# Dilated queries and keys of a two-layer hybrid attention kernel: transposed as 32-bit rows of two heads, split afterwards

## The chip, the cores and the metric

The kernel runs on one core of one Trainium2 chip. The metric is device time in microseconds (us), the median of the runs of one kernel. The engines are called by their names here; in the profile they are PE (TensorE), PEld (TensorE's weight loads), DVE (VectorE), ACT (ScalarE), POOL (GpSimd) and SP (SyncE, which issues all the DMAs that this text speaks of).

## The reference, cut to what matters

Two layers, each on 2048 tokens of width 1024. A layer normalizes its input, multiplies it with one weight matrix and cuts the result into queries, keys, values and gates of two attentions: stick-breaking (4 heads of 64) and dilated windows (12 heads of 64, three patterns). The part that matters is the road from the projection to the dilated attention:

```python
qd = _partial_rope(_rmsnorm(heads(qd, N_HEADS_DIL), q_norm_g[layer]), pos)
kd = _partial_rope(_rmsnorm(heads(kd, N_HEADS_DIL), k_norm_g[layer]), pos)
od = _dilated_mixture(qd, kd, heads(vd, N_HEADS_DIL))
```

`_rmsnorm` divides each head's 64 values by their root mean square and multiplies them with a gain, `_partial_rope` rotates the first 16 of them by the token's position. `_dilated_mixture` then needs scores of queries against keys, so both must lie with the head's 64 values on the partitions.

## The kernel before, in words

The sequence is cut into 16 token tiles of 128. Products of float32 precision are made from float32r matmuls: each operand is split into a rounded high part and the rest, and three products are summed (`mm3`, lines 310 to 312, 128x512 each here).

In a layer `Project.run` works through blocks of 512 columns of the weights: one of stick-breaking queries and keys ("sq"), three of dilated ones ("qk": 256 columns of queries and 256 of keys, so 4 heads of each), then values and gates. A block is 8 groups of two token tiles; a group is 8 x 3 = 24 matmuls for each tile, 48 in all, into two PSUM banks (ring `pm`, four banks). So there are 3 x 8 = 24 "qk" groups in a layer and 48 in the kernel. At the end of a block the next block's weights are loaded (line 228) and split (lines 234 on ScalarE, 235 on VectorE), two k steps at a time, in two raw buffers.

Each "qk" group ends in `qk_out`. The square of the projection (ScalarE, line 361) and its sum over a head (VectorE, 362) give the norm, GpSimd makes the reciprocal root (135, 138), VectorE multiplies (366), GpSimd multiplies with the gain (371) and rotates (378 to 381) in the SBUF tile `qn`, which holds 2 token tiles x 8 heads x 64 values. Then, for each token tile, ScalarE rounds `qn` into the high half of a tile `q2` (line 385) and VectorE writes the rest into its low half (386), so that a head's 64 high and 64 low values lie side by side. For each head and token tile TensorE transposes these 128 columns (line 395), which puts high over low on the partitions, four transposes into one PSUM bank (ring `pt`, four banks). Four evictions follow (397, two on VectorE and two on ScalarE) and four DMAs (399) into the DRAM scratch `qk_scr[pair, 2 queries + 2 keys, 128, 2048]`. The dilated attention reads that scratch later (lines 657 to 666).

The order on each engine is not written out here: a scheduler fixes it before the run from a simulated timeline of the whole kernel, with the exception of the attentions' TensorE work, which is pinned to program order. Waits between engines are semaphores.

Of the kernel before, what the change touches and what calls it, by code (L numbers as in the profile page):

```python
# [10 lines left out]
F32 = mybir.dt.float32  # L11
F32R = mybir.dt.float32r
BF16 = mybir.dt.bfloat16
AF = mybir.ActivationFunctionType
ALU = mybir.AluOpType
# [14 lines left out]
def _constants():  # L30
# [16 lines left out]
    for run, r in ((32, 4), (8, 16)):  # L47
        q = (r * np.arange(run)[None, :] + np.arange(r)[:, None]).reshape(-1)
        cols += [mask(q, q - 128), mask(q, q)]
# [140 lines left out]
class Project:  # L190
# [96 lines left out]
    def run(self, sq_scr, sb_scr, v_scr, qk_scr, g_scr, inject):  # L287
        nc, mem = self.tc.nc, self.mem
# [4 lines left out]
        pm, pt = self.pm, self.pt  # L293
# [7 lines left out]
        r2 = xa[:, 768:1024].rearrange("p (a b c) -> p a b c", a=2, c=16)  # L301
        stg = mem.ring("S0", "S1")
        qnr = mem.ring("H2", "H3")
        q2r = mem.ring("H4", "H5")
        qsr = mem.ring("H0", "H1")
        ssr = mem.ring("U2", "U3")

        def mm3(ps, c, k, wh, wl):
# [48 lines left out]
        def qk_out(i, pss, c):  # L357
            qn = qnr.get([128, 2, 8, 64])
            ss = ssr.get([128, 16])
            for j, ps in enumerate(pss):  # L360
                nc.scalar.activation(qn[:, j].rearrange("p b d -> p (b d)"), ps, AF.Square)
            nc.vector.tensor_reduce(out=ss, in_=qn.rearrange("p a b d -> p (a b) d"),  # L362
                                    op=ALU.add, axis=mybir.AxisListType.X)
            self.rstd_of(ss, ss, 64)
            for j, ps in enumerate(pss):
                nc.vector.tensor_tensor(
                    out=qn[:, j], in0=ps.rearrange("p (b d) -> p b d", d=64),
                    in1=ss[:, 8 * j:8 * j + 8].unsqueeze(2).to_broadcast([128, 8, 64]), op=ALU.mult)
            for s in range(2):
                v = qn[:, :, 4 * s:4 * s + 4]  # L370
                nc.gpsimd.tensor_tensor(
                    out=v, in0=v,
                    in1=gain[:, s].unsqueeze(1).unsqueeze(1).to_broadcast([128, 2, 4, 64]), op=ALU.mult)

            def tb(s, lo, n):
                return tab[:, s, c:c + 2, lo:lo + n].unsqueeze(2).to_broadcast([128, 2, 8, n])

            nc.gpsimd.tensor_tensor(out=r1, in0=qn[:, :, :, 0:16], in1=tb(0, 0, 16), op=ALU.mult)
            nc.gpsimd.tensor_tensor(out=r2[:, :, :, 0:8], in0=qn[:, :, :, 8:16], in1=tb(1, 0, 8), op=ALU.mult)
            nc.gpsimd.tensor_tensor(out=r2[:, :, :, 8:16], in0=qn[:, :, :, 0:8], in1=tb(1, 8, 8), op=ALU.mult)  # L380
            nc.gpsimd.tensor_tensor(out=qn[:, :, :, 0:16], in0=r1, in1=r2, op=ALU.add)
            q2 = []
            for j in range(2):
                t = q2r.get([128, 8, 2, 64], F32R)
                nc.scalar.copy(t[:, :, 0], qn[:, j])
                nc.vector.tensor_tensor(out=t[:, :, 1], in0=qn[:, j], in1=t[:, :, 0].bitcast(F32),
                                        op=ALU.subtract)
                q2.append(t)
            for s in range(2):
                st = qsr.get([128, 2, 2, 256])  # L390
                for m in range(2):
                    ps = pt.get([128, 2, 2, 128], F32R)
                    for h in range(2):
                        for j in range(2):
                            nc.tensor.transpose(ps[:, h, j],  # L395
                                                q2[j][:, 4 * s + 2 * m + h].rearrange("p s d -> p (s d)"), self.ident_r)
                    (nc.scalar.copy if m else nc.vector.tensor_copy)(
                        st[:, m].rearrange("p h t -> p (h t)"), ps.bitcast(F32).rearrange("p h j t -> p (h j t)"))
                    nc.sync.dma_start(
                        out=qk_scr[2 * i + m, 2 * s:2 * s + 2, :, 128 * c:128 * c + 256].rearrange("g p t -> p g t"),  # L400
                        in_=st[:, m])

        self.wt.update({p: mem.get(p, [128, 2048], F32R) for p in ("F2", "F3")})
        wide = [("sq", 0, [(0, QA, 512)])]
# [28 lines left out]
        for bi, (kind, idx, parts) in enumerate(wide):  # L433
            nxt = wide[bi + 1][2] if bi + 1 < len(wide) else None
            for g in range(NT // 2):
# [20 lines left out]
                if kind == "qk":  # L456
                    qk_out(idx, pss, 2 * g)
                    continue
# [3 lines left out]
                for j, ps in enumerate(pss):  # L462
                    st = stg.get([128, 512])
# [3 lines left out]
        for bi, (kind, idx, parts) in enumerate(tail):  # L467
# [9 lines left out]
            for gi, (ct, tq) in enumerate(order):  # L477
# [3 lines left out]
                t = slice(512 * tq, 512 * tq + 512)  # L481
                ps = pm.get([128, 512])
                for k in range(NK):
                    mmw(ps, ct, tq, k, wh[:, k], wl[:, k])
                g = stg.get([128, 512])
# [140 lines left out]
def _dilated(tc, mem, v_scr, qk_scr, g_scr, mix, masks, sel, ident, neg1):  # L626
# [87 lines left out]
    def front(g):  # L714
# [7 lines left out]
        if p:  # L722
            run, stp = (32, 4) if p == 1 else (8, 1)
            w0 = 0 if first else run * (n - 1)
# [262 lines left out]
```

## Time and profile before

| | |
|---|---|
| median of 3 runs | 3177.85 us (3176.13 to 3178.02) |
| profiled execution, own time | 3175.44 us |
| its span, first to last instruction | 3173.7 us |
| mean granted TensorE clock | 0.992 |
| TensorE busy | 3100.5 us, 98% |
| VectorE, ScalarE, GpSimd busy | 51%, 45%, 38% |
| "qk" transposes in the trace, line 395 | 189.7 to 475 us and 1769 to 2054.4 us |

Times of the trace count from the first instruction's start. A row of a timeline has the start in us, the duration in us, the engine, the line of the kernel, the operation, the tiles written and read, and the number of instructions merged into the row; in brackets the idle time before it and what ended it. Matmuls overlap in their pipeline and their ends are modelled, so TensorE's pace is read from one start to the next.

### The profile page before, as it was taken

The page shows a single profiled execution, that of the slowest core. Times are in us where ns is not written, and L with a number is a line of the kernel's source. Part 1 is how long each engine was busy: PE and PEld are TensorE (multiplying, and loading weights), DVE is VectorE, ACT ScalarE, POOL GpSimd, SP SyncE. Part 2 cuts the span into 40 slices and gives each one's busy share as a digit, 9 for nine tenths or more (in the row PEclk, how much of TensorE's full clock was granted, in tenths as well). Part 3 has the DMA queues.
Part 4 walks back from the last instruction along what each step waited for, and adds up shares of the span by engine and source line. Part 5 has one row for each costly group of instructions (what it writes and reads, how often), then busy time and mean ns, then how long its engine had stood idle before and what let it go on. Part 6 is the DMA issues. An engine that isn't in the chain of part 4 may idle for free.

```text
span 3173.7 us, 58878 instructions
## 1 busy us (share of the span) xinstructions
PE 3100.5 (98%) x21712; PEld 2643.9 (83%) x21712; DVE 1618.6 (51%) x4131; ACT 1425.4 (45%) x4013; POOL 1201.7 (38%) x1302
## 2 busy tenths in 40 slices
PE   8999999999999999989999999999999999999899
PEld 8888888987778998868898888888878789888787
DVE  6234440013777888875252344401147778788721
ACT  5223331113667888852042233311136678888410
POOL 1057761002663444451010677511026634454500
PEclk9999999999999999999999999999999999999899
DMA  6333346416223566354443233464162235663443
GB/s 201 91 96 114 112 131 189 129 63 195 75 88 107 151 175 187 114 160 148 125 140 109 90 107 115 145 186 126 50 202 73 89 104 151 194 173 105 145 146 104
DMA packets 313823, 413.15 MB, mean 130 GB/s; under 512 B 20160, under 2 KB 245440, under 8 KB 303296
## 3 DMA queue, kind: packets, MB, share of 16 engines
q1 hardware_dynamic: 313536, 409.38, 42.2%
q8 instruction: 173, 2.83, 0.4%
q14 instruction: 114, 0.93, 0.1%
HBM read 252.01 MB, written 157.29 MB: 129 GB/s over the span
## 4 chain that ended last, share of the span: by engine, by line
PE 87%; DVE 4%; POOL 2%; issue 2%; ACT 2%; DMA 2%; SPq 0%; DVEq 0%; POOLq 0%; ACTq 0%
PE b L311 9%; PE b L310 9%; PE b L312 9%; PE b L737 8%; PE b L772 6%; PE b L758 6%; PE b L316 6%; PE b L318 6%; PE b L317 6%; PE b L940 4%; PE b L941 4%; PE b L937 4%; PE b L597 4%; PE b L583 2%; PE b L395 2%
## 5 line engine op out<-in xcount | busy, mean ns | idle before, releaser
L743 ACT ACTIVATE H<-H,T 128x256 f32<-128x256 f32 (+1 forms) x1152 | 519.3, 455 | 80.6 <-DVE T L739 75.8
L739 DVE CUSTOM_DVE_ANT_0 H<-b,M 128x256 f32<-128x256 f32 (+1 forms) x1152 | 371.0, 360 | 109.6 <-PE b L758 41.4
L737 PE MATMUL b<-F,F 128*128 128x256 f32 (+1 forms) x2304 | 408.2, 301 | 2.8 <-DVE T L739 2.8
L312 PE MATMUL b<-F,F 128*128 128x512 f32 (+1 forms) x1152 | 409.2, 355 | 0.4 <-DVE F L283 0.3
L565 DVE TENSOR_TENSOR_SCAN G<-G,b 128x513 f32<-128x513 f32 (+3 forms) x320 | 324.6, 1079 | 84.8 <-ACT G L564 69.0
L571 POOL TENSOR_TENSOR G<-G 128x512 f32<-128x512 f32 (+3 forms) x320 | 287.9, 913 | 190.8 <-DVE G L565 154.7
L737 PEld LDWEIGHTS b<-F,F 128*128 128x128 f32 x2304 | 312.1, 191 | 31.7 <-issue 26.3
L758 PE MATMUL b<-ident,H 128*128 128x128 f32 x1800 | 298.3, 277 | 5.1 <-ACT H L760 2.6
L311 PE MATMUL b<-F,G 128*128 128x512 f32 (+1 forms) x768 | 274.6, 358 | 0.0
L310 PE MATMUL b<-F,G 128*128 128x512 f32 (+1 forms) x768 | 274.2, 357 | 0.0
L311 PE MATMUL b<-F,F 128*128 128x512 f32 (+1 forms) x768 | 273.4, 356 | 0.0
L310 PE MATMUL b<-F,F 128*128 128x512 f32 (+1 forms) x768 | 272.1, 354 | 0.0
L312 PEld LDWEIGHTS b<-F,F 128*128 128x128 f32 x1152 | 217.6, 189 | 30.8 <-DVE F L283 0.8
L760 DVE COPY H<-b 128x512 f32<-128x512 f32 (+1 forms) x432 | 241.5, 559 | 1.2 <-PE b L758 0.9
L135 POOL TENSOR_SCALAR U<-U 128x16 f32<-128x16 f32 (+1 forms) x80 | 33.1, 414 | 535.5 <-DVE U L362 315.2
L772 PE MATMUL b<-H,H 128*64 128x128 f32 x3600 | 235.8, 278 | 0.0
L317 PE MATMUL b<-F,F 128*128 128x512 f32 x576 | 224.5, 390 | 0.0
L564 ACT ACTIVATE G<-b 128x512 f32<-128x512 f32 (+3 forms) x320 | 164.0, 558 | 133.0 <-PE b L557 105.8
L758 PEld LDWEIGHTS b<-ident,H 128*128 128x128 f32 x1800 | 211.7, 141 | 14.4 <-ACT H L743 6.1
L772 PEld LDWEIGHTS b<-H,H 128*64 128x64 f32 x3600 | 193.2, 137 | 32.0 <-issue 22.4
L743 ACT ACTIVATION_READ_ACCUMULATOR H<-H,T 128x1 f32 x1152 | 219.3, 190 | 0.0
L487 DVE TENSOR_TENSOR S<-b,S 128x512 f32<-128x512 f32 x64 | 44.3, 692 | 318.8 <-ACT S L486 318.8
(159 smaller groups left out, 6636.4 us busy)
## 6 DMA issues: line engine op xcount, KB each, us to landing
qk_l<-H SPq DMA_DIRECT2D x192, 256.0 KB
F<-qk_l SPq DMA_DIRECT2D x48, 1024.0 KB
v_l<-S SPq DMA_DIRECT2D x288, 128.0 KB
H<-v_l SPq DMA_DIRECT2D x72, 512.0 KB
F<-qk_l SPq DMA_DIRECT2D x48, 512.0 KB
sq_l<-H SPq DMA_DIRECT2D x64, 256.0 KB
g_l<-S SPq DMA_DIRECT2D x64, 256.0 KB
F<-sq_l SPq DMA_DIRECT2D x32, 512.0 KB
```

The lines of the kernel that those rows point to most:

```text
L310: nc.tensor.matmul(ps, hT(q, 0, k)[:, cs], wh, start=k == 0, stop=False)
L311: nc.tensor.matmul(ps, hT(q, 0, k)[:, cs], wl, start=False, stop=False)
L312: nc.tensor.matmul(ps, hT(q, 1, k)[:, cs], wh, start=False, stop=k == NK - 1)
L317: nc.tensor.matmul(ps, wh[:, w], hT(tq, 1, k), start=False, stop=False)
L565: nc.vector.tensor_tensor_scan(out=r[:, 0:n + 1][:, ::-1], data0=g[:, 512 - n:513][:, ::-1], data1=z[:, 0:1].to_broadcast([128, n + 1]), i ...
L571: nc.gpsimd.tensor_tensor(out=b[:, :n], in0=r[:, 1:n + 1], in1=r[:, 0:n], op=ALU.subtract)
L737: pin(nc.tensor.matmul(sc[:, h, :un], qb, kv, start=s == 0, stop=s == 1))
L739: nc.vector.tensor_tensor_reduce(out=pe[:, h, :un], in0=sc[:, h, :un], in1=mk[:, m0:m0 + un], scale=-0.125, scalar=3.0e38, op0=ALU.add, op ...
L743: nc.scalar.activation(pe[:, h, :un], pe[:, h, :un], AF.Exp, scale=-1.0, bias=st[:, 0, p, h, b:b + 1], accum_out=st[:, 1, p, h, b:b + 1])
L758: pin(nc.tensor.transpose(tp[:, ch, h], pe[:, h, 128 * w:128 * w + 128], ident))
L760: (nc.scalar.copy if g % 4 == 1 else nc.vector.tensor_copy)(ts[:, :nch], tp[:, :nch])
L772: pin(nc.tensor.matmul(ob[64 * h:64 * h + 64, b % 4], vq[(pr * 3 + p) * 2 + (b - ch) // 8][:, (b - ch) % 8, 64 * h:64 * h + 64], ts[:, ch, h],
```

## The change: what it does

`qn` is no longer split. TensorE transposes it as plain float32, with the float32 identity: 128 columns are now two heads of 64, for one token tile. A group makes 8 such transposes, four into each of two PSUM banks. The split is made when a bank is evicted: ScalarE's copy rounds to the high part `hi`, VectorE subtracts it from the bank and gets `lo`. Each DMA takes 64 partitions (one head) of `hi` or `lo` for two pairs and writes it to the rows where the scratch wants it, high over low; there are eight of these in a group, each of 64 x 2 x 256 values. The scratch has the same content and layout as before. The buffers H4 and H5, which held `q2`, now make up the second halves of the rings of `hi` and `lo`.

```diff
-        q2r = mem.ring("H4", "H5")
-        qsr = mem.ring("H0", "H1")
+        qsr = mem.ring("H0", "H4")
+        qsl = mem.ring("H1", "H5")
...
-            q2 = []
-            for j in range(2):
-                t = q2r.get([128, 8, 2, 64], F32R)
-                nc.scalar.copy(t[:, :, 0], qn[:, j])
-                nc.vector.tensor_tensor(out=t[:, :, 1], in0=qn[:, j], in1=t[:, :, 0].bitcast(F32),
-                                        op=ALU.subtract)
-                q2.append(t)
             for s in range(2):
-                st = qsr.get([128, 2, 2, 256])
+                hi, lo = qsr.get([128, 2, 256], F32R), qsl.get([128, 2, 256], F32R)
+                ps = pt.get([128, 2, 2, 128])
                 for m in range(2):
-                    ps = pt.get([128, 2, 2, 128], F32R)
-                    for h in range(2):
-                        for j in range(2):
-                            nc.tensor.transpose(ps[:, h, j],
-                                                q2[j][:, 4 * s + 2 * m + h].rearrange("p s d -> p (s d)"), self.ident_r)
-                    (nc.scalar.copy if m else nc.vector.tensor_copy)(
-                        st[:, m].rearrange("p h t -> p (h t)"), ps.bitcast(F32).rearrange("p h j t -> p (h j t)"))
-                    nc.sync.dma_start(
-                        out=qk_scr[2 * i + m, 2 * s:2 * s + 2, :, 128 * c:128 * c + 256].rearrange("g p t -> p g t"),
-                        in_=st[:, m])
+                    for j in range(2):
+                        nc.tensor.transpose(ps[:, m, j], qn[:, j, 4 * s + 2 * m:4 * s + 2 * m + 2].rearrange(
+                            "p h d -> p (h d)"), self.ident)
+                pv = ps.rearrange("p m j t -> p m (j t)")
+                nc.scalar.copy(hi, pv)
+                nc.vector.tensor_tensor(out=lo, in0=pv, in1=hi.bitcast(F32), op=ALU.subtract)
+                for l, x in enumerate((hi, lo)):
+                    for h in range(2):
+                        nc.sync.dma_start(
+                            out=qk_scr[2 * i:2 * i + 2, 2 * s + h, 64 * l:64 * l + 64,
+                                       128 * c:128 * c + 256].rearrange("m p t -> p m t"),
+                            in_=x[64 * h:64 * h + 64].bitcast(F32))
```

## Rows read from the trace of the kernel before

**Rows 1.** The page: span; busy time, share and instructions of TensorE.

```profile
span 3173.7 us, 58878 instructions
...
PE 3100.5 (98%) x21712; PEld 2643.9 (83%) x21712; DVE 1618.6 (51%) x4131; ACT 1425.4 (45%) x4013; POOL 1201.7 (38%) x1302
```

**Rows 2.** Busy by stretch: length, engines' us (instructions), granted clock, DMA share, GB/s.

```profile
180.00:480.00 300.00, 300.00 (x1552) 251.24 (x1552) 136.75 (x191) 94.58 (x167) 206.67 (x191) 1.00 0.35 113
1760.00:2060.00 300.00, 300.00 (x1553) 251.25 (x1552) 136.95 (x191) 95.69 (x167) 205.97 (x191) 1.00 0.34 113
```

**Rows 3.** The chain of waits, 399 to 427 us: shares by line.

```profile
by line: PE b L312 29.2%; PE b L311 29.1%; PE b L310 28.4%; PE b L395 14.1%
```

**Rows 4.** Groups by form, whole run: xcount | busy us, mean ns | idle before, releasers.

```profile
L395 PE MATMUL b<-ident_r,H 128*128 128x128 f32 x768 | 71.0, 246 | 0.0
...
L397 DVE COPY H<-b 128x512 f32<-128x512 f32 x96 | 62.3, 686 | 19.8 <-PE b L395 19.8
...
L386 DVE TENSOR_TENSOR H<-H,H 128x512 fp32r<-128x512 f32 x96 | 61.8, 685 | 4.4 <-ACT H L385 4.4
...
L397 ACT COPY H<-b 128x512 f32<-128x512 f32 x96 | 56.1, 588 | 97.1 <-PE b L395 69.4 <-issue 23.5 <-DMA H<-in_w_in 3.8
...
L283 DVE TENSOR_TENSOR F<-b,F 128x512 fp32r<-128x512 f32 x32 | 20.8, 685 | 7.3 <-ACT F L282 7.2
...
L282 ACT CAST F<-b 128x512 fp32r<-128x512 f32 x32 | 17.1, 593 | 19.8 <-PE b L280 19.6
```

**Rows 5.** Timeline of TensorE around a block of line 395.

```profile
412.10 1.48 PE L395 MATMUL b<-ident_r,H 128*128 128x128 f32 x16
413.42 0.46 PE L311 MATMUL b<-F,G 128*128 128x512 f32 x1
413.72 0.40 PE L312 MATMUL b<-F,G 128*128 128x512 f32 x1
413.95 0.39 PE L310 MATMUL b<-F,G 128*128 128x512 f32 x1
```

**Rows 6.** Timeline of TensorE around float32 transposes of the input's preparation, line 280.

```profile
36.26 1.04 PE L280 MATMUL b<-ident,H 128*128 128x128 f32 x8
37.05 0.36 PE L312 MATMUL b<-F,F 128*128 128x256 f32 x1
37.25 0.28 PE L310 MATMUL b<-F,F 128*128 128x256 f32 x1
37.37 0.28 PE L311 MATMUL b<-F,F 128*128 128x256 f32 x1
```

**Rows 7.** Timeline of TensorE in the dilated attention: float32 transposes, line 758.

```profile
1102.45 0.60 PE L758 MATMUL b<-ident,H 128*128 128x128 f32 x4
1102.81 0.76 PE L737 MATMUL b<-F,F 128*128 128x256 f32 x4
```

**Rows 8.** Timeline, 417 to 425 us, all engines: from the rotation to the transposes.

```profile
416.82 0.75 POOL L381 TENSOR_TENSOR H<-X 128x256 f32<-128x256 f32 x1
...
419.32 1.29 DVE L386 TENSOR_TENSOR H<-H,H 128x512 fp32r<-128x512 f32 x2
...
419.49 0.57 POOL L135 TENSOR_SCALAR U<-U 128x16 f32<-128x16 f32 x1 [1.92 <-DVE U L362]
...
424.38 0.79 PE L395 MATMUL b<-ident_r,H 128*128 128x128 f32 x8
```

**Rows 9.** Issues of line 399: duration ns min/median/max, first and last start.

```profile
L399 SPq DMA_DIRECT2D qk_l<-H x192: 359/422/1102, 191.3 to 2057.4; - x192
```

**Rows 10.** Timeline, 252 to 263 us, all engines: a block's end, the next weights.

```profile
256.31 0.19 PEld L310 LDWEIGHTS b<-F,G 128*128 128x128 f32 x1
...
256.96 6.37 SPq L228 DMA_DIRECT2D H<-in_w_in  x9
...
261.33 0.69 DVE L235 TENSOR_TENSOR F<-H,F 128x512 fp32r<-128x512 f32 x1 [0.99 <-ACT F L234]
```

**Rows 11.** TensorE's waits over the run: us in total, times, longest us.

```profile
PE b L583 <- POOL G L571: 16.0, 17, 3.7
```

## The prediction

> **What bounds the kernel now.** I read the page first. TensorE is busy nearly all of the span and no other engine reaches two thirds of it [rows 1]. That is an average over stages, so I next took the two stretches, one in each layer, in which the dilated queries and keys are projected: in both, TensorE is busy for 300.00 of 300 us at a granted clock of 1.00, the upper of its two levels, while VectorE, ScalarE and GpSimd are busy for 46, 32 and 69% and the DMA engines for about 35% [rows 2]. The chain of waits through this stretch consists of TensorE alone, the projection's three matmul lines and the transposes of line 395 [rows 3]. In the table of groups by form these transposes have no idle time in front of them in either layer [rows 4]. So one thing is to be seen: TensorE streams without a break, and a group lasts as long as its instructions. What the change takes from TensorE here is taken from the end; what it takes from ScalarE, VectorE or the queues is worth nothing unless it now delays TensorE.
>
> **The change part by part, TensorE.** A group issues 48 projection matmuls and then, before, 16 transposes of 128x128; after, 8. There are 3 blocks of 8 groups in each of 2 layers, so 48 groups; the 768 transposes of the table are 48 times 16 [rows 4]. The old block is priced from starts, since ends are modelled. It starts at 412.10, the first matmul behind it at 413.42, the second at 413.72 [rows 5]. Two undisturbed matmuls are 0.23 apart, so the block takes 413.72 - 412.10 - 0.23 = 1.39 us: 1.32 for 16 transposes (82 ns each) and 0.07 for the switch back.
>
> The new block holds float32 transposes with the float32 identity. The kernel has these already, in the preparation of the input, between matmuls of the same kind, and eight in a row: start 36.26, first matmul behind at 37.05, second at 37.25, matmuls there 0.12 apart [rows 6]. That is 37.25 - 36.26 - 0.12 = 0.87 us: 0.79 for 8 (99 ns each, so dearer than the old ones) and 0.08 for the switch. I take 0.87, because shape, count and neighbours are the same. The lower bound is the dilated attention's block of four, 1102.81 - 1102.45 = 0.36, or 90 ns each [rows 7], which makes 8 x 0.090 + 0.08 = 0.80. The upper bound is a block that the scheduler cuts into two of four, with two switches: 0.79 + 2 x 0.08 = 0.95. The old blocks in the rows stand uncut, so I do not expect that.
>
> A rule of the Trainium skill speaks against these prices: the page "FP8 and Floating Point Precision", section "TensorE Precision Notes", says that true FP32 takes four passes through the array. By it the sum would turn from a gain into a loss (first rival). The page "TensorE: Matmul & The Clock Gate", section "Terms", names a transpose mode that is four times faster for FP32. The row of 99 ns agrees with the second and not with the first.
>
> **ScalarE, VectorE, GpSimd.** A group loses two splits on ScalarE and two on VectorE (685 ns), made from SBUF, and its four evictions of PSUM (686 ns on VectorE, 588 on ScalarE) turn into two rounding copies on ScalarE and two subtractions on VectorE. The new pair has the form of lines 282 and 283, at 593 and 685 ns [rows 4]. So ScalarE and VectorE each do two instructions fewer, some 1.2 us (2 x 0.59) and 1.4 us (2 x 0.69) in each group. TensorE covers that: none of it counts. If TensorE were not in front of everything here, the 1.4 us would be its worth. GpSimd's work is unchanged.
>
> **The order and the wait that moves.** The transposes used to wait for VectorE's second split; now they wait for GpSimd's last addition of the rotary part. In one group that addition ends at 416.82 + 0.75 = 417.57, the splits at 419.32 + 1.29 = 420.61, and the transposes start at 424.38 [rows 8]. The data is thus ready 3.8 us before it is used, and the step removed is 3.0 us long. The scheduler may place the new block up to about those 3.0 us earlier and keep 3.8 us, or leave it and have 6.8. Behind a TensorE that waits there all matmuls of the next group would queue. I cost this at nothing. Eviction now runs in a line (copy 0.59, subtraction 0.69) instead of side by side, some 0.6 us longer. The PSUM banks of the transposes are four, and a group now needs two of them instead of four, so none is late.
>
> **SyncE's queue and the DMAs.** The four writes of a group become eight of half the size, still rows of 1 KB, so bytes and packets stay. An issue of line 399 has a median of 422 ns [rows 9]; eight are 3.4 us in a group of about 12. The queue is in order, and at three block ends in a layer the next weights are queued behind these writes: there the loads start at 256.96, the last split of them ends at 262.02, and the group that uses it began near 256.3 [rows 10]. It needs that last piece after 7 of its 8 steps, 42 matmuls of 0.23, near 265.8. Four more issues cost 4 x 0.42 = 1.7 us and the longer eviction 0.6, within the 3.8 us that are free. Nothing, then; if that cover were gone, up to about 2 us at each of 6 places, 12 us.
>
> **The sum.** 48 x (1.39 - 0.87) = 48 x 0.52 = 25.0 us less. With the lower bound 48 x 0.59 = 28.3, with the upper 48 x 0.44 = 21.1. The profiled execution took 3175.44 us, 1.7 beside its span of 3173.7, so it would take 3150.5. The three timed runs have a median of 3177.85, 2.4 above it; I forecast for that median 3153, between 3149 and 3157.
>
> **The rivals.**
> First, that a float32 transpose streams its columns four times when it stands in this stage. Then 128 columns cost what a 512-column matmul costs, 0.23 us; eight are 1.84 and with the switch 1.92, so the block is 0.53 longer and the kernel 48 x 0.53 = 25 us slower, 3203. This decides once a transpose costs more than (1.39 - 0.08) / 8 = 164 ns. For it speaks the operand's type; against it all rows of float32 transposes here. 3 in 100.
>
> Second, that TensorE waits for GpSimd. The order is fixed beforehand from modelled times. If the removed splits were modelled as longer than 6.8 us after GpSimd's end, the block would now be placed ahead of its data, and each us of wait costs 48. It outweighs the saving from 0.52 us of wait; 1 us would give 3201. Related to it, VectorE's new subtractions can fall in front of the multiply of line 366, for which GpSimd waits; GpSimd idles 1.92 us in front of line 135 in each group [rows 8], of which a group shortened by 0.52 leaves 1.4, and the two subtractions take 1.4. For it: GpSimd is the next busiest engine. Against: 3.8 us of slack. 8 in 100, half of it a smaller gain (3157 to 3171), half no gain or a loss.
>
> Third, that the doubled issues delay the weights at the block ends, up to 12 us given back: 3157 to 3165. Against it is the slack of 3.8. 9 in 100.
>
> Fourth, that the scheduler, which orders the unpinned work of the whole kernel from one simulated timeline, arranges something else anew. TensorE idles little elsewhere: its longest sum of waits is 16.0 us over the whole run [rows 11]. Some us either way; 6 in 100 that this leads out of the forecast's band, mostly to 3140 to 3149.
>
> **How the numbers follow.** The forecast has 74 in 100. The range that leaves out 2 in 10 adds the third rival and the nearer part of the second and fourth: 3145 to 3164. What a measurement of this kernel can tell from no change is about 0.2%, 6.4 us, so faster means below 3171.5. Faster: 74 + 4 of the second + 9 + 4 of the fourth = 91. Slower: 3 + 3 = 6. The same: 3.
>
> **What would show it.** The table by form should have 384 float32 transposes in blocks of 8, with 0.79 us from the first to the next matmul; the stretches of 300 us should hold more groups (period about 11.8 instead of 12.3), TensorE still at 300.00. Wrong would be: idle time in front of the transposes with GpSimd as releaser (second rival), idle time at a block's first group with a split or a weight load as releaser (third), 8 transposes that take 1.8 us (first).

## The result, and the profile after

The changed kernel takes 3153.67 us (median of 6 runs, 3152.62 to 3159.12); the kernel before, over 6 runs by then, 3175.95. The ratio is 0.9934, with a 95% interval of 0.9922 to 0.9946: 22.3 us less. Forecast were 3153, a range of 3145 to 3164 and 25.0 us less.

In the changed file `qk_out` is shorter, so the transposes are line 387, the rounding copies 390, the subtractions 391, the writes 394, and later lines stand 4 lower. First the page of the profile after, which answers to [rows 1] (this execution took 3159.12 us, one of the longer ones):

```profile
PE 3079.0 (98%) x21328; PEld 2620.1 (83%) x21328; DVE 1559.6 (49%) x4035; ACT 1372.0 (43%) x3917; POOL 1171.5 (37%) x1302
```

TensorE has 384 instructions less, half of 768, and is still busy for 98% of the span of 3157.4 us. The stretch in layer 1 that answers to [rows 2], in the same columns:

```profile
180.00:480.00 300.00, 300.00 (x1412) 248.43 (x1411) 109.03 (x143) 68.71 (x119) 191.98 (x191) 1.00 0.46 116
```

TensorE never stops here, and the clock is the same; in layer 2 (1760 to 2060 us) it is again 300.00 us at 1.00. VectorE fell from 46 to 36%, ScalarE from 32 to 23%. One number moved that should not have: the DMA share rose from 0.35 to 0.46 (in layer 2 from 0.34 to 0.48), though the bytes of the whole run stayed (409.4 MB in both pages; more on it below). The timeline of TensorE around a block, which answers to [rows 5]:

```profile
401.06 1.03 PE L387 MATMUL b<-ident,H 128*128 128x128 f32 x8
401.86 0.48 PE L310 MATMUL b<-F,G 128*128 128x512 f32 x1
402.18 0.40 PE L311 MATMUL b<-F,G 128*128 128x512 f32 x1
```

From the block's start to the first matmul behind it are 401.86 - 401.06 = 0.80 us, and the gap from that matmul to the second is 402.18 - 401.86 - 0.23 = 0.09 longer than usual. Together that is 0.89 by these rounded rows, and 0.88 in the mean of the trace's 48 blocks. The block before this one starts at 389.26, so the period is 11.80 us; before it was 424.38 - 412.10 = 12.28 [rows 5, 8]. That is 0.48 less, and 48 groups make 23.0.

The sharpest reading is the length of the stage, from the first of its 128x512 matmuls of line 310 to the end of the last. Its two ends after, in layer 1:

```profile
160.29 0.40 PE L310 MATMUL b<-F,G 128*128 128x512 f32 x1
...
532.27 0.39 PE L310 MATMUL b<-F,F 128*128 128x512 f32 x1
```

532.27 + 0.39 - 160.29 = 372.37 us. The same two ends before:

```profile
160.45 0.40 PE L310 MATMUL b<-F,G 128*128 128x512 f32 x1
...
543.99 0.39 PE L310 MATMUL b<-F,F 128*128 128x512 f32 x1
```

543.99 + 0.39 - 160.45 = 383.93 us. Layer 2 gives the same two lengths. So the stage lost 11.56 us in each layer, 23.1 in all, and that is the result. The table of the experiments uses this length; the stage contains the values' block too (8 groups that did not change).

### The profile page after: what moved, and what is told of

Its sections match the earlier page's. It is cut to its first block, busy times and chain, and to the rows that moved or that the text cites. A ratio compares the mean times of both kernels' runs of the same rounds, so it can differ in the third digit from the quotient of the medians.

```text
span 3157.4 us, 58152 instructions
## 1 busy us (share of the span) xinstructions
PE 3079.0 (98%) x21328; PEld 2620.1 (83%) x21328; DVE 1559.6 (49%) x4035; ACT 1372.0 (43%) x3917; POOL 1171.5 (37%) x1302
## 4 chain that ended last, share of the span: by engine, by line
PE 86%; DVE 4%; ACT 3%; issue 3%; POOL 2%; DMA 2%; SPq 0%; DVEq 0%; POOLq 0%; ACTq 0%
PE b L312 9%; PE b L311 9%; PE b L310 9%; PE b L733 7%; PE b L768 6%; PE b L316 6%; PE b L318 6%; PE b L317 6%; PE b L754 5%; PE b L936 4%; PE b L937 4%; PE b L933 4%; PE b L593 3%; PE b L579 2%; DVE G L561 2%
## 5 line engine op out<-in xcount | busy, mean ns | idle before, releaser
L135 POOL TENSOR_SCALAR U<-U 128x16 f32<-128x16 f32 (+1 forms) x80 | 18.4, 231 | 539.7 <-DVE U L362 317.9
```

## The experiments

The number of runs stands in brackets behind a time.

| kernel | time, us | stage, layer 1 / 2, us |
|---|---|---|
| before | 3175.95 (6) | 383.93 / 383.93 |
| changed | 3153.67 (6) | 372.37 / 372.37 |
| changed once more | 3154.8 (5) | 372.37 / 372.37 |
| transposes twice | 3201.4 (1) | 393.43 / 393.43 |
| plain matmuls | 3201.8 (1) | 393.87 / 393.87 |
| before with half blocks | 3140.07 (1) | 367.53 / 367.53 |
| 16 writes | 3227.18 (4) | 405.10 / 405.61 |
| splits put back | 3152.4 (4) | 372.37 / 372.37 |
| GpSimd longer | 3166.2 (1) | 373.50 / 373.43 |
| 4 writes | 3149.84 (1) | 372.36 / 372.37 |

**The changed kernel once more** (no edit).

> The changed kernel once more. If TensorE's shorter blocks are the whole effect, the median stays near 3153 us, the stage from the first dilated projection to the last value projection is again 372.4 us in each layer (383.9 before), and the executions that took about 3159 differ from the others outside it: the profiled one held a 6.0 us wait of TensorE near 2353 us, where the stick-breaking attention of layer 2 begins. If instead the stage itself varies, its 372.4 will differ between profiles of a long and a short execution.

Median 3154.8 (3153.93 to 3156.72), ratio 0.9938 (0.9924 to 0.9952). The stage has the same length to 0.01 us in a profile of 3157.4 and in one of 3153.1 us of span. The longer one, with `POOL` waiting for the DMA of the attention's selection matrix where the stick-breaking attention of layer 2 begins (waits of GpSimd, then of TensorE, 2317 to 2400 us; us in total, times, longest):

```profile
POOL F L700 <- DMA S<-in_sel: 13.6, 2, 9.9
...
PE b L579 <- POOL G L567: 6.9, 4, 6.0
```

and the shorter one:

```profile
POOL F L700 <- DMA S<-in_sel: 9.8, 2, 5.7
...
PE b L579 <- POOL G L567: 3.0, 4, 1.8
```

A load that lands later holds GpSimd's queue, and TensorE waits behind it. The longest waits differ by 4.2 us on both engines, and the spans by 4.3. Neither wait is at a changed line. Why the load lands later in one execution is open, and so is whether the new order of the kernel has a part in it.

**The transposes made twice.**

```diff
-                        nc.tensor.transpose(ps[:, m, j], qn[...], self.ident)
+                        for _ in range(2):
+                            nc.tensor.transpose(ps[:, m, j], qn[...], self.ident)
```

> Each of the 8 float32 transposes is made twice, with the same result. If TensorE's issued work sets the end, 8 x 99 ns x 48 = 38 us more than the changed kernel, so about 3191. If the block was partly hidden by anything else, less.

The timeline of TensorE:

```profile
402.73 1.91 PE L388 MATMUL b<-ident,H 128*128 128x128 f32 x16
404.40 0.48 PE L312 MATMUL b<-F,F 128*128 128x512 f32 x1
```

From start to first matmul it is 1.67 us now, so the second eight cost 0.87, 109 ns each and not 99. The first eight cost no less. A row of the timeline merges the transposes of a block; the eighth of the changed kernel's block at 401.06, by itself, is

```profile
401.83 0.27 PE L387 MATMUL b<-ident,H 128*128 128x128 f32 x1
```

Seven steps take 401.83 - 401.06 = 0.77 us, 0.11 each, and the matmul behind starts only 401.86 - 401.83 = 0.03 after the last transpose. The time that this short step leaves out comes back in the long gap to the second matmul, which was read as a switch. So the price of a transpose is 0.11 us in blocks of 8 and of 16; 0.09 in a block of four [rows 7] and 0.10 in one of eight [rows 6] came from a division by a count that includes the short last step. The whole block, up to the usual pace, was priced rightly.

The stage grew by 21.06 us in a layer, 42.1 in all, and 24 x 0.87 = 20.9 is that growth. Every added transpose is seen in the time, so nothing covered the block. The total rose by 46.6 against the median of the run above; the other 4.5 lie outside the stage, within what single executions differ by.

**Plain matmuls with the identity.**

```diff
-                        nc.tensor.transpose(ps[:, m, j], qn[...], self.ident)
+                        nc.tensor.matmul(ps[:, m, j], qn[...], self.ident, start=True, stop=True)
```

> The same 8 products with the identity, as ordinary float32 matmuls and not as transposes. If four passes are the price of the operand's type unless the transpose mode is on, 8 take about 8 x 0.227 = 1.8 us and not 0.79: 48 us more than the changed kernel, about 3202. If the type alone doesn't cost passes here, nothing changes: 3153.

```profile
403.88 1.95 PE L387 MATMUL b<-ident,H 128*128 128x128 f32 x16
...
405.90 0.39 PE L310 MATMUL b<-F,F 128*128 128x512 f32 x1
```

Eight products stand as 16 records. The second row is the second matmul behind them, so the block takes 405.90 - 403.88 - 0.23 = 1.79 us: 0.224 for a product, against 0.88 / 8 = 0.110 for a transpose. A product of 128 columns thus costs what a float32r matmul of 512 columns does (0.227). The Trainium skill says that true FP32 takes four passes through the array ("FP8 and Floating Point Precision", "TensorE Precision Notes"). The price of the product agrees with it, and that of a transpose of the same operands, half as much, does not. That passes alone make these prices is not shown: a product also has two weight loads for a transpose's one, and even a float32r transpose costs 1.39 / 16 = 0.087 us, more than a quarter of 0.227. Written this way the change would have been a loss: the stage would be longer than before.

**The kernel before with half of its transposes.**

```diff
-                        for j in range(2):
+                        for j in range(1):
                             nc.tensor.transpose(ps[:, h, j], ...)
...
+                        st[:, m].rearrange("p h (j t) -> p h j t", j=2),
+                        ps[:, :, 0:1].bitcast(F32).to_broadcast([128, 2, 2, 128]))
```

> The kernel before with only the first of two token tiles transposed (8 float32r transposes in a block and not 16) and its copy written twice, so half of the queries and keys are wrong. If count and price per transpose explain all, a block takes 8 x 82 = 0.66 us and the time falls by 48 x 0.66 = 31.6 us against the kernel before, about 3144; the difference of some 6.5 us to the changed kernel is then what float32 costs over float32r. If the gain came from the removed splits and waits, less than 20 us.

```profile
410.99 0.80 PE L395 MATMUL b<-ident_r,H 128*128 128x128 f32 x8
411.62 0.47 PE L311 MATMUL b<-F,G 128*128 128x512 f32 x1
411.92 0.39 PE L312 MATMUL b<-F,G 128*128 128x512 f32 x1
```

Half of the transposes are left out here. By these rows a block of eight float32r transposes takes 411.92 - 410.99 - 0.23 = 0.70 us, and 0.71 in the mean of the 48 blocks. The stage lost 16.40 us in each layer. Halving the count is worth 32.8 us, and float32 in place of float32r costs 2 x (372.37 - 367.53) = 9.7 of them; 23.1 are left. Of the 9.7, 48 x (0.88 - 0.71) = 8.2 are the blocks, the rest the slower matmuls behind them. The whole data in float32r was not tried: rounded to it, the tile would lose the low part that the change splits off afterwards.

**Sixteen writes.**

```diff
-                        nc.sync.dma_start(out=qk_scr[2 * i:2 * i + 2, ...], in_=x[64 * h:64 * h + 64])
+                        for m in range(2):
+                            nc.sync.dma_start(out=qk_scr[2 * i + m, ...], in_=x[64 * h:64 * h + 64, m])
```

> The changed kernel with each of its eight writes of a group cut in two, so 16 DMAs of 64 KB and the same bytes. If SyncE's queue and the DMAs are hidden, the stage from the first dilated projection to the last value projection stays at 372.4 us in each layer and the ratio to the changed kernel is 1.000. If the doubled issues already cost something at the block ends, doubling them again costs at least as much once more: 8 x 0.42 = 3.4 us at each of 6 places, up to 20 us.

3227.18 us, ratio to the kernel before 1.0158 (1.0143 to 1.0173): 73.5 us above the changed kernel. Both sides of the expectation were too low. The timeline of SyncE's queue:

```profile
271.10 10.04 SPq L395 DMA_DIRECT2D qk_l<-H  x16
```

Sixteen issues occupy the queue for 10.04 of the 11.8 us of a group, and the next weights stand behind them, from 281.18 on. TensorE's waits, 160 to 570 us:

```profile
PE b L310 <- ACT F L234: 17.2, 3, 8.2
PE b L310 <- DVE H L366: 8.0, 2, 5.2
```

The first is the split of the weights at the block ends, as the third rival had it, and it is 8.2 us long at its worst. The second is a PSUM bank of the projection that is not read yet. These waits make 25.2 of the 32.7 us that layer 1 lost. Most of the rest is the clock: behind each of the three longest, of 5.2, 7.0 and 8.2 us, the granted clock stood at 0.50, the lower level (284.5 to 289.5 us for one), and the matmuls started 0.43 us apart instead of 0.23. That makes 32 starts late, by 6.8 us in all.

**The splits put back.**

```diff
+            for j in range(2):
+                t = q2r.get([128, 512], F32R)
+                nc.scalar.copy(t, qn[:, j])
+                nc.vector.tensor_tensor(out=t, in0=qn[:, j], in1=t, op=ALU.subtract)
```

> The changed kernel with the removed work of ScalarE and VectorE put back: both splits of each group are made again from the unsplit tile, into a tile that nothing reads. If only TensorE's blocks count, nothing changes: about 3154, the stage 372.4. If the relief of ScalarE and VectorE had a part in the gain, up to 1.2 to 1.4 us a group come back, as much as 60 us, and in any case more than 6.

```profile
180.00:480.00 300.00, 300.00 (x1412) 248.44 (x1411) 136.66 (x191) 94.04 (x167) 204.55 (x191) 1.00 0.46 116
```

VectorE and ScalarE are as busy as before the change, and the stage is 372.37 us. The time is 3152.4, ratio to the kernel before 0.9922 (0.9905 to 0.9938). Their relief is worth nothing.

**GpSimd longer.**

```diff
+            for _ in range(4):
+                junk = jr.get([128, 2, 8, 16])
+                nc.gpsimd.tensor_tensor(out=junk, in0=r1, in1=r2, op=ALU.add)
             nc.gpsimd.tensor_tensor(out=qn[:, :, :, 0:16], in0=r1, in1=r2, op=ALU.add)
```

> The changed kernel with four more additions on GpSimd in each group, written to a tile that nothing reads, ahead of the last one: 4 x 0.74 = 3.0 us. GpSimd idles 2.1 us in front of line 135 in each group of 11.8. If that is the whole slack of its round, a group becomes 0.8 us longer, 48 x 0.8 = 40 us, with idle time of TensorE in front of the transposes or the projections; if the round has more slack than that, nothing changes and the stage stays 372.4.

```profile
180.00:480.00 300.00, 299.40 (x1406) 247.29 (x1405) 111.02 (x143) 65.18 (x118) 259.82 (x287) 1.00 0.45 113
```

Neither: GpSimd is busy for 87% and the stage grew by 1.1 us in a layer, where 20 were expected if 2.1 us were the whole slack. The edit put the four additions ahead of the rotation's last one, but the scheduler did not leave them there: of the 96 in the stretch, 28 run behind the next group's line 138, where GpSimd had idled 1.47 us ahead of line 371 in the changed kernel. With the 2.1 us ahead of line 135 the round thus has some 3.6 us of idle time, and the rotation was still done 1.6 us or more before every block. So the second rival was farther off than its rows suggested. The total, of one execution, is 11.4 above the repeated run; some 9 of it lie outside the stage and are not explained.

**Four writes.**

```diff
-                hi, lo = qsr.get([128, 2, 256], F32R), qsl.get([128, 2, 256], F32R)
+                hl = qsr.get([128, 2, 2, 256], F32R)
+                hi, lo = hl[:, :, 0], hl[:, :, 1]
...
+                for m in range(2):
+                    nc.sync.dma_start(
+                        out=qk_scr[2 * i + m, 2 * s:2 * s + 2, :, 128 * c:128 * c + 256].rearrange("g p t -> p g t"),
+                        in_=hl[:, m].bitcast(F32))
```

> The changed kernel with high and low parts side by side in one tile and the four writes of 128 partitions and 256 KB that the kernel before made. The rows land in another order than the attention expects, so the output is another. If the count of writes is hidden, the stage stays at 372.4 us and the time near 3154; if eight writes cost something, it falls by up to 12 us.

```profile
180.00:480.00 300.00, 300.00 (x1412) 248.47 (x1410) 109.95 (x144) 68.70 (x119) 192.35 (x191) 1.00 0.37 119
```

The stage is 372.36 us. Eight writes cost nothing over four. That one execution was 3149.84 us, 1.1 below the shortest of the kernels with the stage's same length; the difference lies outside the stage, and one execution does not settle it.

## Why the prediction was right, point by point

- **TensorE alone sets the time of the stage.** Shown from three sides: what was added to the block came out in full (transposes twice), what was put back on ScalarE and VectorE came out as nothing, and TensorE was busy for 300.00 of 300 us before and after.
- **The price of the blocks.** Predicted were 1.39 us before and 0.87 after, 0.52 less. The blocks measured 1.39 and 0.88, 0.51 less, and the period fell by 0.48. The other 0.03 is a tail: the matmuls behind a float32 block start up to 0.24 apart for about nine starts, not 0.23. This term was some 1.9 us too large over 48 groups (25.0 against 23.1). That float32 costs more than float32r for each transpose, and that half the count outweighs it, held: 32.8 less, 9.7 back. The parts within the block were misread: a transpose costs 109 ns and not 99, there is hardly a switch, and the lower bound from a block of four [rows 7] was no lower price. The sum did not suffer, because it used the whole block.
- **The time itself.** That 3153 was met within 0.7 us is in part luck. The saving was forecast 2.7 us too large, and the three runs that it was taken from had a median 1.9 us above that of all six.
- **First rival, four passes.** Its price was near (predicted 0.23 for a product, measured 0.224), its condition was not met: `transpose` does not pay it. But the prediction read the 99 ns as agreeing with the transpose mode that the Trainium skill calls four times faster for FP32 ("TensorE: Matmul & The Clock Gate", "Terms"). Measured is a factor of two, 0.224 against 0.110, so the row agreed with neither rule in full.
- **Second rival, a wait for GpSimd.** The rotation now ends at 395.58 + 0.74 = 396.32 and the block starts at 401.06, 4.7 us later, between the 3.8 and 6.8 that were given; at the ends of the blocks of columns it is as little as 3.3, less than either. The timeline of all engines, answering to [rows 8]:

```profile
395.58 0.74 POOL L381 TENSOR_TENSOR H<-X 128x256 f32<-128x256 f32 x1
...
398.44 0.20 POOL L135 TENSOR_SCALAR U<-U 128x16 f32<-128x16 f32 x1 [2.12 <-DVE U L362]
```

GpSimd idles 2.1 us ahead of line 135, no less than before. VectorE's subtractions (from 402.87 us) come behind the multiply of line 366 (from 401.67), so they are not in GpSimd's way.

- **Third rival, SyncE's queue.** Hidden, as forecast, but the cost was mis-sized. An issue is dearer than the 0.42 us that were carried over from the larger write [rows 9]:

```profile
L394 SPq DMA_DIRECT2D qk_l<-H x384: 574/597/2018, 189.6 to 2036.8; - x192
```

Eight are 4.8 us by the median, not 3.4, in a group of 11.8. That is 3.1 more than the four before, not 1.7; with the 0.6 of the eviction it is 3.7 of the 3.8 us that were counted as free, so by its own count the term of nothing held with next to nothing to spare. The run with 16 shows that the cover ends between 8 and 16 writes.
- **Fourth rival, the order elsewhere.** Some us, of either sign: the profiled execution is only 16.3 us shorter than the one before, since 6.8 of the stage's 23.1 went to other places, above all to the wait near 2353 us (TensorE's waits from 2300 to 2500 us sum to 4.1 us more than before). The medians, 22.3 apart, show that this is not the rule.

## What to carry to other kernels

Where TensorE streams without a gap, count what each edit adds to or takes from its queue, and price the whole block from starts of the same form in the same trace, up to where the next matmuls have their usual pace again; a price for one instruction, divided out of a short block, can mislead. The splits and evictions on other engines then need no price, only a check that they stay ahead. Transposing before a split into two parts halves the transposes, even if each one becomes dearer, as long as it is made as a transpose and not as a product. A queue that is hidden today is worth a count of its issues: here twice the writes were free, and four times the writes cost three times the gain.

## What the runs showed of the hardware

- The issue of a write from 64 partitions took 597 ns by the median, of one from 128 partitions with twice the bytes 422 (469 in the run with four writes), of one from 64 partitions with half the bytes (the run with 16) 594. With the half-width writes the DMA engines were busy for 46% of the stretch at 116 GB/s, with four full-width ones for 37% at 119: the same bytes kept them longer.
- Float32 transposes of 128x128 start 108 to 110 ns apart in blocks of 8 and of 16; float32r ones some 85 apart, after two shorter steps of about 60 at a block's start. The first matmul behind a float32 block starts only 28 ns after the last transpose, the second one 0.32 us after the first.
- The same float32 product as an ordinary matmul costs 0.224 us, twice the transpose's 0.110.
- After float32 transposes the following float32r matmuls are slower for about nine starts; after eight float32r transposes only the first one is.
- Behind waits of TensorE of 5.2, 7.0 and 8.2 us in layer 1 of the run with 16 writes the granted clock stood at 0.50, and the matmuls of 512 columns started 0.43 us apart.
